# Six gate tiles in the half-size block instead of four, another layout of k and q in DRAM, and a later product with the softmax reciprocals

## The chip, the cores and the metric

The kernel runs on one core of a Trainium2 chip. The metric is the device time of one execution in microseconds, median of several runs: 974.61 us before (three runs, 974.07 to 975.96). A profile of one more execution is read beside it. The engines are TensorE (PE; PEld is its weight load), VectorE (DVE), ScalarE (ACT), GpSimd (POOL) and SyncE (SP), which only issues DMAs here.

## The reference

One layer of a bidirectional encoder on 512 tokens of width 2048. One projection gives q, k, v and a gate for two groups of 16 heads of 64; group A attends with three dilated windows that share a bias table, group B to a 2-D neighbourhood on an 8 x 64 grid. Gated outputs go through the output projection, and the result is normalised with the scaled input.

```python
h = jnp.einsum('bsd,de->bse', x, w_in[layer])
qa, ka, va, ga, qb, kb, vb, gb = jnp.split(h, splits, axis=-1)
ya = _dilated_attention(heads(qa, N_HEADS_A), heads(ka, N_HEADS_A), heads(va, N_HEADS_A), t5_bias)
yb = _neighbourhood_attention(heads(qb, N_HEADS_B), heads(kb, N_HEADS_B), heads(vb, N_HEADS_B), na_rpb[layer])
ya = merge(ya) * jax.nn.silu(ga.astype(jnp.float32))
yb = merge(yb) * jax.nn.silu(gb.astype(jnp.float32))
y = jnp.concatenate([ya, yb], axis=-1).astype(x.dtype)
out = jnp.einsum('bse,ed->bsd', y, w_out[layer])
x = _layer_norm(DEEPNORM_ALPHA * x + out, ln_gain[layer], ln_bias[layer])
```

## The kernel before

Everything is float32, and each product is made of three TensorE passes on rounded high and low parts: high x high, high x low, low x high. ScalarE makes a high part with a copy, VectorE the low part with a subtraction.

**Stages.** First `plain_block` computes the first four of 16 gate tiles (a tile is 128 gate columns, the gate of one pair of heads) while x arrives. Then `strassen_block` computes k, q and v of both groups, one block for each kind and group, with Strassen's scheme: seven products of half-size matrices instead of eight. Between k and q of group B stands a block of kind "s", with half-size operands, for the next `MID` = 4 gate tiles. The other eight gate tiles are computed later, as fillers in the attention loop.

**Units.** A block's products are cut into units of weights. A unit is loaded by SP (`load`), summed with another unit where the product needs it (`add`, VectorE), split into a high part (`high`, ScalarE) and a low part (`low`, VectorE), and multiplied (`run`, TensorE). `run_blocks` lays them out by hand: at unit n it issues the sum of unit n+3, the split of n+2 and the matmuls of n; `behind` holds what else is due there, such as the combining of products, the stores, and the loads, which go out some units ahead (`base - ahead`). A k or q result leaves in eight pieces (`store_kq`), each turned by TensorE, split, and stored to DRAM by SP. PE, DVE and ACT follow this order as written; SP's order is made by the scheduler, in one queue for loads and stores.

**The loop.** Each of the 16 pairs of heads (groups alternate) has eight steps, four for a head of 128 queries each. At step n the loop (lines 813 to 851) issues: the scores of n (two matmuls into a bank of the pool `pss`, which has two banks); the softmax's first instruction on VectorE (s, with the row minimum) and the exponential on ScalarE; the transposes of step n-2 (`turn`), which ScalarE and VectorE copy out as th and tl; and at n % 4 == 2 the value matmuls of the head before (`values`, into the same pool), which ScalarE copies (tmp) and VectorE adds (y). Between these it puts matmuls that need nothing of the step, the fillers: `fill(amount)` takes them from the remaining gate tiles and then from the first half of the output projection (`out_first`). In a step, half of `amount` goes ahead of `turn`, the rest behind. `later` puts a task behind a step; VectorE's tasks of steps with n % 4 == 1 are held until the next step's softmax has been issued (`held`).

**A pair's y.** `share` (n % 8 == 1 of the next pair) turns the softmax sums' reciprocals and sends them through DRAM (`rc_d`) to a tile rc, `gate` (n % 8 == 4) multiplies y by the gate, and `gated` (n % 8 == 7) by rc, and then makes y's high (ScalarE) and low part (VectorE) for the output projection, one step after the other. `load_kq`, `load_v`, `load_sg` and `load_bias` fetch what the next pair needs; k's high and low parts lie on the two halves of the partitions, q's high part is put there twice, and its low part (`ql`) lies beside zeros.

Of the kernel before, what the change touches and what calls it, by code (L numbers as in the profile page):

```python
# [64 lines left out]
ORDER = [(m % 2, m // 2) for m in range(2 * PAIRS)]  # L65
EARLY, MID = 4, 4
AWAKE = 9
# [4 lines left out]
def hybrid_layer(tc, xT, xn, w_in, w_early, w_mid, w_gate, w_out, t5x, brow, rpb, cmask, eye, gain, lbias, out):  # L72
    nc = tc.nc
    from contextlib import ExitStack
    with ExitStack() as ctx:
# [154 lines left out]
        def store_kq(kind, g, ch, half, b, src):  # L230

            o = vst.next("kst", F32R)
            hi, lo = o[:, 0:512], o[:, 512:1024]
            if kind == "k":
                split(src, hi, lo)
            else:
                nc.scalar.activation(hi, src, AF.Copy, scale=-0.125)
                nc.vector.scalar_tensor_tensor(lo, src, -0.125, f(hi), op0=ALU.mult, op1=ALU.subtract)
            o = o.rearrange("p (s n q) -> p s n q", s=2, n=2)
            for n in range(2):  # L240
                for i in range(2):
                    if kind == "k":
                        to = k_d[g][4 * ch + 2 * b + n].rearrange("s c a q -> c s a q")[:, :, i]
                        nc.sync.dma_start(to[:, :, HALF * half:HALF * half + HALF], f(o[64 * i:64 * i + 64, :, n]))
                    else:
                        to = q_d[g][4 * ch + 2 * b + n][i].rearrange("c (b h q) -> c h b q", b=4, h=2)[:, half]
                        nc.sync.dma_start(to, f(o[:, i, n].rearrange("p (b q) -> p b q", b=4)))

# [102 lines left out]
        def strassen_block(src, kind, g, hooks):  # L351

            base = len(jobs)
            units, tiles = (2, 1) if kind == "s" else (4, 2)

            def load(q, tags):
                def run():
                    for u in range(units):
                        raw = slot(tags[u], F32, "braw")
                        nc.sync.dma_start(raw, src[units * q + u])  # L360
                        raws[q].append(raw)
                return run
# [3 lines left out]
            def product(i, pool, q, other=None, onto=None):  # L366
# [7 lines left out]
                def high(u):  # L374
                    h = halves.next("wh", F32R)
                    nc.scalar.activation(h, raws[q][u], AF.Copy)  # L376
                    return h

                def low(u, h):
                    l = halves.next("wl", F32R)  # L380
                    nc.vector.tensor_tensor(l, raws[q][u], f(h), ALU.subtract)  # L381
                    return h, l

                def run(u, h, l):
                    if u == 0 and first:
                        accs.extend(bank(pool, "acc") for _ in range(tiles))
                    if kind == "s":
                        for kk in range(4):
                            k = 4 * u + kk
                            ah, al = operand(i, k)  # L390
                            for n in range(2):
                                c = slice(256 * kk + 128 * n, 256 * kk + 128 * n + 128)
                                o = accs[0][:, HALF * n:HALF * n + HALF]
                                nc.tensor.matmul(o, h[:, c], ah, start=first and k == 0 and n == 0, stop=False, skip_group_check=skip)
                                nc.tensor.matmul(o, h[:, c], al, start=False, stop=False, skip_group_check=skip)
                                nc.tensor.matmul(o, l[:, c], ah, start=False, stop=k == 7 and n == 1, skip_group_check=skip)
                    for t in range(2 if kind != "s" else 0):
# [24 lines left out]
            def pair(name):  # L422
                if name not in made:
                    t = temps.next(name)
                    made[name] = [t[:, :512], t[:, 512:]]
                return made[name]
# [8 lines left out]
            tags = list(sets)  # L435
            if kind == "s":
                for q, ahead, i, m in ((0, 6, 0, 0), (1, 5, 0, 2), (3, 3, 1, 0), (2, 0, 1, 2)):
                    behind.setdefault(base - ahead, []).append(load(q, tags[i][m:m + 2]))
            else:
                for q, ahead, i in ((0, 6, 0), (1, 4, 1), (3, 2, 2)):  # L440
                    behind.setdefault(base - ahead if base else -4, []).append(load(q, tags[i]))
                at(2, 2, load(2, tags[1]))

# [29 lines left out]
            def put(name, ch, half, t):  # L473
                o = p1[t] if name == "c11" else pair(home[name])[t]
                if kind == "v":
                    store_v(g, ch, half, t, o)
                    return
                sg = vst.next("sg")[:, :512]
                silu(sg, o)
                for n in range(2):  # L480
                    nc.sync.dma_start(sg_d[EARLY + 2 * ch + n][:, HALF * half:HALF * half + HALF], sg[:, HALF * n:HALF * n + HALF])

# [323 lines left out]
        with tc.manual_schedule(engines=engines):  # L806
# [224 lines left out]
def _weights(w_in, w_out):  # L1031
# [20 lines left out]
    for i in range(2):  # L1052
        for j in range(2):
            a = np.concatenate([w[8 * i:8 * i + 8, :, c:c + 128] for c in gate[EARLY + 2 * j:EARLY + 2 * j + 2]], axis=2)
            mid.append(a.reshape(2, 4, 128, 256).transpose(0, 2, 1, 3).reshape(2, 128, 1024))
    return (np.concatenate(blocks), early, np.concatenate(mid), np.concatenate([narrow(c) for c in gate[EARLY + MID:]]),
# [37 lines left out]
```

## Time and profile before

| | |
|---|---|
| median of 3 runs | 974.61 us (974.07 to 975.96) |
| the profiled execution: its own time | 975.21 us |
| its span in the profile | 973.4 us |
| TensorE / VectorE / ScalarE / GpSimd instructions | 4789 / 1144 / 857 / 323 |
| DMA | 194.18 MB, mean 199 GB/s |

The profile covers one execution. Busy times of an engine are given per stage in windows counted from the span's start. Matmuls overlap, so that the mean duration of one is not the time that it takes out of TensorE's queue; for that, starts are compared. "<-" names what ended an idle time.

### The profile page before, as it was taken

The numbers are of one execution on the slowest core, as the hardware profiler recorded it, in microseconds if no ns is written. First come the engines' busy times: TensorE is split into PE (matmuls) and PEld (weight loads), VectorE is DVE, ScalarE is ACT, GpSimd is POOL, SyncE is SP. The second block draws the span as 40 slices with busy tenths as digits, with TensorE's granted clock in tenths as the row PEclk, the third lists the DMA queues.
The fourth block names the chain that finished last, engine by engine and source line by source line (L and its number), as shares of the span: only waits on it lengthen the run. The fifth ranks groups of instructions, "written<-read, shape, count | busy, mean of one in ns | idle before, by whom it ended". The sixth has DMA issues, their size and how long they took to land. (4 is left out here: it accounts for less than half of the span.)

```text
span 973.4 us, 13993 instructions
## 1 busy us (share of the span) xinstructions
PE 964.3 (99%) x4789; PEld 803.6 (83%) x4789; DVE 757.0 (78%) x1144; ACT 496.3 (51%) x857; POOL 181.3 (19%) x323
## 2 busy tenths in 40 slices
PE   8999999999999999999999999999999999999997
PEld 6887888888888889988888888888888888888886
DVE  7897778679789777796788856777776777777877
ACT  7454444444444344443445446776766766672300
POOL 1006656835636000000000000011111000100020
PEclk9999999999999999999999999999999999999999
DMA  9715796698396087420872687887887678779213
GB/s 336 277 65 133 229 329 210 171 296 235 107 350 207 33 282 206 163 93 17 266 182 103 206 271 209 224 234 212 236 239 218 204 228 204 209 219 314 91 58 117
DMA packets 120263, 194.18 MB, mean 199 GB/s; under 512 B 49455, under 2 KB 69807, under 8 KB 120192
## 3 DMA queue, kind: packets, MB, share of 16 engines
q1 hardware_dynamic: 107520, 169.68, 57.3%
q0 software_dynamic: 12096, 22.95, 8.5%
q8 instruction: 38, 0.62, 0.3%
q10 hardware_dynamic: 576, 0.66, 0.2%
q14 instruction: 33, 0.27, 0.1%
HBM read 148.69 MB, written 44.50 MB: 198 GB/s over the span
## 5 line engine op out<-in xcount | busy, mean ns | idle before, releaser
L376 ACT ACTIVATE wh<-braw 128x1024 fp32r<-128x1024 f32 x182 | 193.3, 1062 | 269.2 <-PE acc L404 206.5
L381 DVE TENSOR_TENSOR wl<-braw,wh 128x1024 fp32r<-128x1024 f32 x182 | 223.6, 1230 | 53.8 <-ACT wh L376 53.6
L403 PE MATMUL acc<-wh,xk 128*128 128x512 f32 x384 | 151.3, 394 | 0.0
L405 PE MATMUL acc<-wl,xk 128*128 128x512 f32 x384 | 149.7, 390 | 0.0
L404 PE MATMUL acc<-wh,xk 128*128 128x512 f32 x384 | 149.5, 389 | 0.0
L372 DVE TENSOR_TENSOR braw<-braw 128x1024 f32<-128x1024 f32 x104 | 126.6, 1217 | 0.1
L403 PE MATMUL acc<-wh,op 128*128 128x512 f32 x288 | 113.1, 393 | 0.0
L405 PE MATMUL acc<-wl,op 128*128 128x512 f32 x288 | 112.2, 390 | 0.0
L404 PE MATMUL acc<-wh,op 128*128 128x512 f32 x288 | 112.1, 389 | 0.0
L756 PE MATMUL acc<-wh,yk 128*128 128x512 f32 x320 | 108.1, 401 | 0.0
L692 DVE TENSOR_TENSOR tl<-pt,th 128x256 fp32r<-128x256 f32 (+1 forms) x128 | 71.0, 555 | 35.8 <-ACT th L691 34.1
L691 ACT ACTIVATE th<-pt 128x256 fp32r<-128x256 f32 (+1 forms) x128 | 62.3, 489 | 47.6 <-PE pt L686 45.4
L403 PEld LDWEIGHTS acc<-wh,xk 128*128 128x128 f32 x384 | 72.1, 188 | 15.3 <-ACT bias L151 0.9
L405 PEld LDWEIGHTS acc<-wl,xk 128*128 128x128 f32 x384 | 72.1, 188 | 15.2
L404 PEld LDWEIGHTS acc<-wh,xk 128*128 128x128 f32 x384 | 72.2, 188 | 14.5
L627 ACT ACTIVATE p<-s,mn 128x512 f32<-128x512 f32 (+1 forms) x96 | 62.2, 648 | 29.4 <-DVE mn L623 29.0
L623 DVE CUSTOM_DVE_ANT_0 s<-sc,biases 128x512 f32<-128x512 f32 (+2 forms) x128 | 67.7, 529 | 10.8 <-PE sc L667 10.0
L562 PE MATMUL acc<-xk,wh 128*128 128x512 f32 x256 | 75.3, 404 | 0.0
L756 PEld LDWEIGHTS acc<-wh,yk 128*128 128x128 f32 x320 | 58.5, 189 | 8.8
L161 POOL DMA_DIRECT2D bias<-rows_d x128 | 61.6, 489 | 17.6 <-DMA biasa_d<-bias 5.5
L756 PE MATMUL acc<-wl,yk 128*128 128x512 f32 x160 | 63.9, 403 | 0.0
L405 PEld LDWEIGHTS acc<-wl,op 128*128 128x128 f32 x288 | 54.1, 188 | 11.4
(188 smaller groups left out, 1708.2 us busy)
## 6 DMA issues: line engine op xcount, KB each, us to landing
braw<-in_w_in SPq DMA_DIRECT2D x96, 512.0 KB
wraw<-in_w_out SPq DMA_DIRECT2D x32, 512.0 KB
k_d<-kst SPq DMA_DIRECT2D x64, 128.0 KB
q_d<-kst SPq DMA_DIRECT2D x64, 128.0 KB
v_d<-vst SPq DMA_DIRECT2D x32, 256.0 KB
q<-q_d SPq DMA_DIRECT2D x32, 256.0 KB
wraw<-in_w_gate SPq DMA_DIRECT2D x16, 512.0 KB
k<-k_d SPq DMA_DIRECT2D x16, 512.0 KB
```

The source lines that it names most:

```text
L372: nc.vector.tensor_tensor(raws[q][u], raws[q][u], raws[other][u], ALU.add)
L376: nc.scalar.activation(h, raws[q][u], AF.Copy)
L381: nc.vector.tensor_tensor(l, raws[q][u], f(h), ALU.subtract)
L403: nc.tensor.matmul(accs[t], ah[:, q], h[:, c], start=first and k == 0, stop=False, skip_group_check=skip)
L404: nc.tensor.matmul(accs[t], al[:, q], h[:, c], start=False, stop=False, skip_group_check=skip)
L405: nc.tensor.matmul(accs[t], ah[:, q], l[:, c], start=False, stop=k == 7, skip_group_check=skip)
L562: nc.tensor.matmul(acc, w[:, k * 128:k * 128 + 128], X[8 * u + k][:, s], start=u == 0 and n == 0 and k == 0, stop=u == 1 and n == 2 and k ...
L623: nc.vector.tensor_tensor_reduce(*flat, bias, 1.0, 3e38, ALU.add, ALU.min, mn)
L627: nc.scalar.activation(p[:, to:to + n].rearrange("p (b r c) -> p b r c", r=8, c=c), s[:, :n].rearrange(order, r=8, c=c), AF.Exp, bias=mn, ...
L691: nc.scalar.activation(th, pt[:, :nch], AF.Copy)
L692: nc.vector.tensor_tensor(tl, pt[:, :nch], f(th), ALU.subtract)
L756: nc.tensor.matmul(acc[:, part], yk[k][:, s, c], w[:, wk], start=first and kk == 0 and n == 0, stop=last and kk == 1 and n == 2)
```

## The change

- `MID` goes from 4 to 6: the block "s" computes six gate tiles, and six are left as fillers. The block's units become four per product with 2 x 384 columns instead of two with 4 x 256, and a result has two accumulators (512 and 256 wide). Its loads go out at the same units as those of the other blocks.
- In DRAM k's high and low parts, and q's two heads, lie next to each other for each of the 64 channels. A pair's k is one load as before, q's high part one load on 128 partitions (each row read twice) instead of two on 64, and ql a load onto every second partition, of a tile that is zero elsewhere. A piece of q is stored by eight DMAs of 64 partitions instead of four of 128.
- The fillers are 6, 5, 1, 4 in each four steps until step 75 and 8, 6, 1, 6 then (before: 8, 6, 1, 6 until step 63 and 8, 7, 1, 7). In steps with n % 4 == 1 until step 75 one filler, not half, stands ahead of the transposes.
- `gated` runs at n % 8 == 1 of the pair after the next, two steps later, but for the last two pairs.

```diff
-EARLY, MID = 4, 4
+EARLY, MID = 4, 6
...
-        k_d = [dram.tile([PAIRS, 2, 64, 2, S], F32, name=f"k{g}_d") for g in range(2)]
-        q_d = [dram.tile([PAIRS, 2, 128, S], F32, name=f"q{g}_d") for g in range(2)]
+        k_d = [dram.tile([PAIRS, 64, 2, 2, S], F32, name=f"k{g}_d") for g in range(2)]
+        q_d = [dram.tile([PAIRS, 2, 64, 2, S], F32, name=f"q{g}_d") for g in range(2)]
...
                     else:
-                        to = q_d[g][4 * ch + 2 * b + n][i].rearrange("c (b h q) -> c h b q", b=4, h=2)[:, half]
-                        nc.sync.dma_start(to, f(o[:, i, n].rearrange("p (b q) -> p b q", b=4)))
+                        to = q_d[g][4 * ch + 2 * b + n][i].rearrange("c a (b h q) -> c a h b q", b=4, h=2)[:, :, half]
+                        for a in range(2):
+                            nc.sync.dma_start(to[:, a], f(o[64 * a:64 * a + 64, i, n].rearrange("p (b q) -> p b q", b=4)))
...
-            units, tiles = (2, 1) if kind == "s" else (4, 2)
+            units, tiles = 4, 2
+            cols, wide = (128 * MID // 2, (512, HALF * (MID // 2 - 2))) if kind == "s" else (512, (512, 512))
...
-                        for kk in range(4):
-                            k = 4 * u + kk
+                        for kk in range(2):
+                            k = 2 * u + kk
                             ah, al = operand(i, k)
-                            for n in range(2):
-                                c = slice(256 * kk + 128 * n, 256 * kk + 128 * n + 128)
-                                o = accs[0][:, HALF * n:HALF * n + HALF]
...
+                            for n in range(MID // 2):
+                                c = slice(cols * kk + 128 * n, cols * kk + 128 * n + 128)
+                                o = accs[n // 2][:, HALF * (n % 2):HALF * (n % 2) + HALF]
...
-            nc.gpsimd.memset(f(ql[64:128]), 0.0)
+            nc.gpsimd.memset(f(ql), 0.0)
...
-            nc.sync.dma_start(f(kt.rearrange("p a n -> p (a n)")), k_d[g][j].rearrange("s c a q -> (s c) (a q)"))
-            for n, to in enumerate((qt[0:64], qt[64:128], ql[0:64])):
-                nc.sync.dma_start(f(to), q_d[g][j][n // 2].rearrange("(a c) q -> c a q", a=2))
+            nc.sync.dma_start(f(kt.rearrange("p a n -> p (a n)")), k_d[g][j].rearrange("c s a q -> (c s) (a q)"))
+            nc.sync.dma_start(f(qt.rearrange("p a n -> p (a n)")), _view(q_d[g], j * 256 * S, [[2 * S, 64], [0, 2], [1, 2 * S]]))
+            nc.sync.dma_start(f(ql[0:128:2].rearrange("p a n -> p (a n)")), q_d[g][j][1].rearrange("c a q -> c (a q)"))
...
-                amount = ((8, 6, 1, 6) if n < 64 else (8, 7, 1, 7))[b]
+                amount = ((6, 5, 1, 4) if n < 76 else (8, 6, 1, 6))[b]
+                ahead = 1 if b == 1 and n < 76 else amount // 2
...
-                    fill(amount // 2)
+                    fill(ahead)
...
-                    fill(amount - amount // 2)
+                    fill(amount - ahead)
...
-                if n >= 8 and n % 8 == 7:
+                if n % 8 == 1 and 2 <= i < 2 * PAIRS:
+                    gated(i - 2)
+                if n % 8 == 7 and i >= 2 * PAIRS - 1:
                     gated(i - 1)
```

Line numbers behind the first edit are up to three apart before and after. Three places of the built program show how instructions move.

SP's queue in the stretch in which the block q of group A ends and v begins; `kst` is a piece of q, `braw` are weights. Before:

```order
L360 DMA braw<-in_w_in 128x1024 x6
L247 DMA q_d<-kst 512x1x64 x4
L360 DMA braw<-in_w_in 128x1024
L247 DMA q_d<-kst 512x1x64 x4
L360 DMA braw<-in_w_in 128x1024 x7
L247 DMA q_d<-kst 512x1x64 x4
L360 DMA braw<-in_w_in 128x1024
L247 DMA q_d<-kst 512x1x64 x4
L360 DMA braw<-in_w_in 128x1024
L247 DMA q_d<-kst 512x1x64 x16
L360 DMA braw<-in_w_in 128x1024 x4
```

and now:

```order
L362 DMA braw<-in_w_in 128x1024 x6
L248 DMA q_d<-kst 64x4x64 x16
L362 DMA braw<-in_w_in 128x1024 x2
L248 DMA q_d<-kst 64x4x64 x8
L362 DMA braw<-in_w_in 128x1024 x4
L248 DMA q_d<-kst 64x4x64 x8
L362 DMA braw<-in_w_in 128x1024 x4
L248 DMA q_d<-kst 64x4x64 x32
L362 DMA braw<-in_w_in 128x1024 x4
```

Ahead of the ninth to twelfth of these weight loads stood eight q stores; now 24 smaller ones stand there.

TensorE in a step with n % 8 == 1 of the loop, from its scores to the next step's value matmuls; `acc` rows are fillers, the `pt` rows with `biases` the transposes. Before:

```order
L667 MATMUL sc<-k,ql 128x512
L562 MATMUL acc<-xk_111,wl 128x512
L562 MATMUL acc<-xk_112,wl 128x512
L562 MATMUL acc<-xk_113,wl 128x512
L686 MATMUL pt<-ident,biases 128x128 x2
L562 MATMUL acc<-xk_98,wh 128x512
L562 MATMUL acc<-xk_99,wh 128x512
L562 MATMUL acc<-xk_100,wh 128x512
L717 MATMUL pt<-ident,den 8x128
L666 MATMUL sc<-k,q 128x512
L667 MATMUL sc<-k,ql 128x512
L708 MATMUL pv<-th,vv 128x256 x3
```

and now:

```order
L666 MATMUL sc<-k,ql 128x512
L561 MATMUL acc<-xk_105,wl 128x512
L685 MATMUL pt<-ident,biases 128x128 x2
L561 MATMUL acc<-xk_106,wh 128x512
L561 MATMUL acc<-xk_107,wh 128x512
L561 MATMUL acc<-xk_108,wh 128x512
L561 MATMUL acc<-xk_109,wh 128x512
L716 MATMUL pt<-ident,den 8x128
L665 MATMUL sc<-k,q 128x512
L666 MATMUL sc<-k,ql 128x512
L707 MATMUL pv<-th,vv 128x256 x3
```

One filler instead of three stands ahead of the transposes, and four instead of three between them and the value matmuls that read their copies.

VectorE around the start of a pair of group A; `ISA s,mn` is the softmax's first instruction, the row with `rc` the product with the reciprocals, the row with `pv` the addition behind the value matmuls. Before:

```order
L739 TENSOR_TENSOR y<-y,rc 128x512
L623 ISA s,mn<-sc,biases 128x512
L623 ISA mn 128x1
L692 TENSOR_TENSOR tl<-pt,th 128x256
L844 RECIPROCAL den<-den 128x8
L623 ISA s,mn<-sc,biases 128x512
L623 ISA mn 128x1
L692 TENSOR_TENSOR tl<-pt,th 128x256
L623 ISA s,mn<-sc,biases 128x512
L623 ISA mn 128x1
L548 TENSOR_TENSOR wl<-wraw,wh 128x1024
L741 SCALAR_TENSOR_TENSOR yk<-y,yk 128x512
```

and now:

```order
L622 ISA s,mn<-sc,biases 128x512
L622 ISA mn 128x1
L691 TENSOR_TENSOR tl<-pt,th 128x256
L622 ISA s,mn<-sc,biases 128x512
L622 ISA mn 128x1
L738 TENSOR_TENSOR y<-y,rc 128x512
L833 TENSOR_TENSOR y<-pv,tmp 64x512
L691 TENSOR_TENSOR tl<-pt,th 128x4x128
L622 ISA s,mn<-sc,biases 128x512
L622 ISA mn 128x1
L691 TENSOR_TENSOR tl<-pt,th 128x4x128
L740 SCALAR_TENSOR_TENSOR yk<-y,yk 128x512
```

The product with rc has moved from in front of the pair's first softmax to behind its third, directly ahead of the addition of y; y's low part (`yk`) has moved from there to behind the fourth step's tl.

More of the change, by code (lines that the diff above doesn't have):

```diff
@@ L358, in run @@
                     for u in range(units):
[L359 removed]
+                        raw = slot(tags[u], F32, "braw")[:, :2 * cols]
                         nc.sync.dma_start(raw, src[units * q + u])
@@ L374, in high @@
                 def high(u):
-                    h = halves.next("wh", F32R)
+                    h = halves.next("wh", F32R)[:, :2 * cols]
                     nc.scalar.activation(h, raws[q][u], AF.Copy)
@@ L379, in low @@
                 def low(u, h):
-                    l = halves.next("wl", F32R)
+                    l = halves.next("wl", F32R)[:, :2 * cols]
                     nc.vector.tensor_tensor(l, raws[q][u], f(h), ALU.subtract)
@@ L385, in run @@
                     if u == 0 and first:
-                        accs.extend(bank(pool, "acc") for _ in range(tiles))
+                        accs.extend(bank(pool, "acc")[:, :n] for n in wide)
                     if kind == "s":
-                        for kk in range(4):
-                            k = 4 * u + kk
+                        for kk in range(2):
+                            k = 2 * u + kk
                             ah, al = operand(i, k)
-                            for n in range(2):
-                                c = slice(256 * kk + 128 * n, 256 * kk + 128 * n + 128)
-                                o = accs[0][:, HALF * n:HALF * n + HALF]
-                                nc.tensor.matmul(o, h[:, c], ah, start=first and k == 0 and n == 0, stop=False, skip_group_check=skip)
+                            for n in range(MID // 2):
+                                c = slice(cols * kk + 128 * n, cols * kk + 128 * n + 128)
+                                o = accs[n // 2][:, HALF * (n % 2):HALF * (n % 2) + HALF]
+                                nc.tensor.matmul(o, h[:, c], ah, start=first and k == 0 and n % 2 == 0, stop=False, skip_group_check=skip)
                                 nc.tensor.matmul(o, h[:, c], al, start=False, stop=False, skip_group_check=skip)
-                                nc.tensor.matmul(o, l[:, c], ah, start=False, stop=k == 7 and n == 1, skip_group_check=skip)
+                                nc.tensor.matmul(o, l[:, c], ah, start=False, stop=k == 7 and (n % 2 == 1 or n == MID // 2 - 1),
+                                                 skip_group_check=skip)
                     for t in range(2 if kind != "s" else 0):
@@ L424, in pair @@
                     t = temps.next(name)
-                    made[name] = [t[:, :512], t[:, 512:]]
+                    made[name] = [t[:, :512], t[:, 512:512 + wide[1]]]
                 return made[name]
@@ L435, in strassen_block @@
             tags = list(sets)
[L436 to L442, printed above, removed]
+            for q, ahead, i in ((0, 6, 0), (1, 4, 1), (3, 2, 2)):
+                behind.setdefault(base - ahead if base else -4, []).append(load(q, tags[i]))
+            at(2, 2, load(2, tags[1]))
             def keep(t):
@@ L477, in put @@
                     return
-                sg = vst.next("sg")[:, :512]
+                sg = vst.next("sg")[:, :wide[t]]
                 silu(sg, o)
-                for n in range(2):
-                    nc.sync.dma_start(sg_d[EARLY + 2 * ch + n][:, HALF * half:HALF * half + HALF], sg[:, HALF * n:HALF * n + HALF])
+                for n in range(wide[t] // HALF):
+                    nc.sync.dma_start(sg_d[EARLY + MID // 2 * ch + 2 * t + n][:, HALF * half:HALF * half + HALF], sg[:, HALF * n:HALF * n + HALF])
             for t in range(tiles):
```

7 lines of the change are left out of this document (4 added, 3 removed).

## The prediction

> **What bounds the kernel now.** I read the page's busy times first, then the chain that ended last, then busy time by stage, and last who waits for whom inside the attention stage.
>
> ```profile
> PE 964.3 (99%) x4789; PEld 803.6 (83%) x4789; DVE 757.0 (78%) x1144; ACT 496.3 (51%) x857; POOL 181.3 (19%) x323
> PE 26%; DVE 1%; ACT 1%; issue 1%; DMA 1%; DVEq 0%; POOL 0%; ACTq 0%
> ```
>
> TensorE is busy for 964.3 of 973.4 us, and the chain of waits that can be followed back is nearly all TensorE too. A busy share says nothing about rate, because matmuls overlap. So I looked for stages in which TensorE waits at all.
>
> ```profile
> core 0: us, PE busy (x) PEld busy (x) DVE busy (x) ACT busy (x) POOL busy (x), PEclk, DMA share, GB/s
> 50.00:367.00 317.00, 317.00 (x1434) 260.91 (x1433) 256.40 (x257) 144.95 (x168) 140.34 (x252) 1.00 0.67 205
> 367.00:409.00 42.00, 42.00 (x351) 41.87 (x351) 31.69 (x34) 18.79 (x22) 0.00 (x0) 1.00 0.63 192
> 409.00:563.00 154.00, 154.00 (x696) 127.47 (x695) 126.09 (x130) 72.27 (x85) 1.90 (x2) 1.00 0.48 142
> 576.00:720.00 144.00, 143.78 (x782) 119.31 (x781) 105.71 (x252) 99.86 (x238) 15.26 (x28) 1.00 0.82 229
> 720.00:880.00 160.00, 159.83 (x867) 133.09 (x866) 117.86 (x272) 108.67 (x257) 13.35 (x26) 1.00 0.76 215
> ```
>
> The stages are the projection blocks (50 to 563, with the half-size gate block at 367 to 409) and the attention loop's first 64 steps and the rest (576 to 880). TensorE is covered everywhere, at a granted clock of 1.00. So a change gains what it takes out of TensorE's queue, and loses what it makes TensorE wait. VectorE has the least room: 256 of 317 us in the blocks, 106 of 144 in the loop.
>
> **The change part by part. First, the move of two gate tiles.** In the half-size block the sum over k runs through 7 products of 8 k-tiles, and each column chunk of 128 takes 3 matmuls on 256 positions (high x high, high x low, low x high). Four tiles are 2 chunks, 7 x 8 x 2 x 3 = 336 matmuls; six are 3 chunks, 504. As a filler a tile is 48 matmuls on 512 positions, so 96 of these go.
>
> ```profile
> L394 PE MATMUL acc<-xk,wh x64: 278/283/364, 367.6 to 408.5; 128*128 128x256 f32 x64
> L396 PE MATMUL acc<-xk,wl x64: 279/283/283, 367.9 to 408.8; 128*128 128x256 f32 x64
> 690.37 0.44 PE pt L686 x4
> 880.31 15.67 PE acc L756 x69
> ```
>
> The durations of 283 ns overlap and can't be used. From the first start to the last there are 41.2 us; one more interval, less two bursts of four transposes for the k block before it (0.44 us each by the like burst of the chain), leaves 40.4 us for 336: 0.1205 us each. On 512 positions the chain has 69 in 15.67 us: 0.227 each, and fillers cost the same. The block grows by 168 x 0.1205 = 20.2 us, the fillers shrink by 96 x 0.227 = 21.8 us (22.1 at 0.23): **-1.7 us**. This is the whole arithmetic gain. A tile costs 10.1 us in the block and 10.9 as a filler; at the long matmul's rate seven products for eight would give 9.5, but a short one costs 6% more per element.
>
> The Trainium skill, page "TensorE: Matmul & The Clock Gate", section "Back-to-back issue gap", puts the gap at N/2.4 + 2.5 ns, 109 ns for 256 columns and 216 for 512. By it the block would grow by 18.3 us and the fillers shrink by 20.7: -2.4 us. The rows here are 10 and 5% above the page, so their -1.7 is used.
>
> Can the block hold that pace? A unit of weights is now 768 wide instead of 1024 and has 18 matmuls, 2.17 us, where it had 24, 2.89 us.
>
> ```profile
> L381 DVE TENSOR_TENSOR wl<-braw,wh 128x1024 fp32r<-128x1024 f32 x14 | 17.0, 1218 | 2.2 <-ACT wh L376 2.2
> L372 DVE TENSOR_TENSOR braw<-braw 128x1024 f32<-128x1024 f32 x104 | 126.6, 1217 | 0.1
> L89 DVE TENSOR_TENSOR wl<-wraw,wh 128x512 fp32r<-128x512 f32 x15 | 10.3, 684 | 0.8 <-ACT wh L88 0.7
> ```
>
> At 768 wide an instruction lies halfway between 684 and 1218, 0.95 us by estimate. The block then has 28 low parts and 16 sums, 42 us, and 18 combining and gating steps of at most 0.7 us each: 54 of its 60.7 us. A unit with a sum needs 1.9 of 2.17 us; the projection blocks run at 2.43 of 2.72 (12 x 0.227) with no wait of TensorE. So I cost the pace at nothing, hidden by work prepared two units ahead. If that cover went, each of the 16 units with a sum could last 0.2 us longer: +3 us. The bytes are the same: the weights of two tiles, four loads of 512 KB, move from the gate stream to the block. The zero fill of 128 partitions instead of 64 is on GpSimd, which is idle there.
>
> **Second, the loop with fewer fillers.** The 49 fillers of the prologue stay. Steps 0 to 75 have 16 per four steps instead of 21 (22 from step 64), and the rest 21 instead of 22. In the first 64 steps that is 80 fillers, 18.2 us less cover. VectorE loses only 80/24 = 3.3 low parts of 1.2 us and one gate product, some 4.7 us. From 105.7 of 144 us it goes to about 101 of 126, so 25 us of idle time are left. What is its idle time now?
>
> ```profile
> engine line waited for: us in total, times, longest us
> DVE tl L692 <- ACT th L691: 16.8, 24, 1.2
> DVE y L833 <- ACT tmp L832: 16.2, 14, 1.7
> DVE s L623 <- PE sc L667: 7.7, 4, 6.0
> DVE y L739 <- DMA rc<-rc_d: 1.2, 2, 0.6
> ```
>
> 33 us are waits for ScalarE's th and tmp, latencies that don't shrink with the fillers. 33 into 25 doesn't go: some 8 us must vanish because VectorE arrives later, or become waits of TensorE. This bounds the new stalls of these steps: 0 to 8 us. Where they would come is seen at one step:
>
> ```profile
> 617.75 0.48 PE L666 MATMUL sc<-k,q 128*128 128x512 f32 x1
> 618.86 0.69 DVE L833 TENSOR_TENSOR y<-pv,tmp 64x512 f32<-64x512 f32 x1 [1.02 <-ACT tmp L832]
> 619.58 0.69 DVE L692 TENSOR_TENSOR tl<-pt,th 128x512 fp32r<-128x512 f32 x1
> 620.12 0.40 PE L666 MATMUL sc<-k,q 128*128 128x512 f32 x1
> 620.19 0.68 DVE L568 SCALAR_TENSOR_TENSOR sgo<-sgo,acc 128x512 f32<-128x512 f32 x1
> 620.78 0.68 DVE L623 CUSTOM_DVE_ANT_0 s<-sc,biases 128x512 f32<-128x512 f32 x1
> ```
>
> y ends at 619.55 and frees the bank that the scores at 620.12 write: 0.57 us to spare. The step between loses two fillers, 0.46 us, so 0.11 is left. Behind the waiting scores stand every later matmul and filler. The scores of 617.75 are taken up 3.0 us later, at 620.78; with steps 0.46 us shorter such lateness grows. The edit that issues one filler, not three, ahead of the second step's transposes gives th two fillers more room, at the one place where TensorE waits for it. Today VectorE runs 3 us late and TensorE loses a few tenths, so I choose near the low end: **+1.6 us** for the loop.
>
> **Third, y times the reciprocals two steps later.**
>
> ```profile
> 680.11 5.90 DMA rc<-rc_d
> 686.03 0.69 DVE L739 TENSOR_TENSOR y<-y,rc 128x512 f32<-128x512 f32 x1 [0.55 <-DMA rc<-rc_d]
> 686.64 0.68 DVE L623 CUSTOM_DVE_ANT_0 s<-sc,biases 128x512 f32<-128x512 f32 x1
> 688.60 0.28 PE L708 MATMUL pv<-th,vv 128*128 128x256 f32 x1
> 689.03 0.63 PE L708 MATMUL pv<-th,vv 128*128 128x256 f32 x3 [0.15 <-ACT th L691]
> ```
>
> The reciprocals land at 686.0, VectorE stands 0.55 us for them, the softmax behind starts late, and a value matmul on 256 positions, due 0.12 us after its neighbour, comes after 0.43: 0.3 us lost. It happens twice in the 16 pairs. Two steps later the DMA is long home. The product also moves into the place where VectorE waits for tmp, while the low part of y moves out of it, to the step before a head starts: no net work moves. I take **-0.8 us** for these and the smaller waits they cause (0 to -1.2). The product ends well before the output projection's fourth unit reads pair 7 at step 77.
>
> **Fourth, k and q in DRAM.** Loads: two of q instead of three for each pair, in rows of 4 KB; they are issued a pair, eight steps, ahead, and that hides them: nothing. If that failed, a pair's scores would wait, but the loads get fewer. Stores of q: eight issues a piece instead of four.
>
> ```profile
> L247 SPq DMA_DIRECT2D q_d<-kst x64: 512/637/3278, 188.9 to 506.3; - x64
> L244 SPq DMA_DIRECT2D k_d<-kst x64: 574/599/1179, 109.6 to 387.3; - x64
> 188.93 2.87 SPq L247 DMA_DIRECT2D q_d<-kst  x4
> 192.57 4.41 SPq L247 DMA_DIRECT2D q_d<-kst  x4
> 197.07 5.27 SPq L360 DMA_DIRECT2D braw<-in_w_in  x7
> 202.43 6.66 SPq L247 DMA_DIRECT2D q_d<-kst  x4
> 215.02 1.22 DVE L372 TENSOR_TENSOR braw<-braw 128x1024 f32<-128x1024 f32 x1
> ```
>
> A half store still has three dimensions like the k store, so about 0.6 us each: 4 x 0.6 = 2.4 us more on SP for each of the eight pieces. The order of SP's queue shows what stands behind: the weight loads of the next block's second set, now in the run of seven from 197.07, come after the third piece, that is after 24 stores. That piece's stores begin at 202.43 today; eight at 0.6 us, or 6.7 us if the queue holds them up as now, end at 207 to 209. VectorE sums the first of these weights at 215.02, and TensorE uses them three units after the sum. So it is hidden, by 6 us less a landing time that SP's rows don't show (the rc load took 5.9). I cost it at nothing, and at +4 us if that cover goes (below).
>
> The Trainium skill, page "DMA: Bandwidth & Descriptors", section "Rules for kernel authors", says that two transfers to disjoint partition halves serialise and that one over 128 partitions is to be used. It speaks for the new q load and against the halved q store: by it the sum would take the +4 us of the rival on SP, by the rows nothing; no run yet shows either.
>
> Sum: -1.7 + 1.6 - 0.8 = **-0.9 us**, made against the profiled execution of 975.21 us (span 973.4, and 1.8 around it); that one lies 0.6 above the median of 974.61, to which I apply the difference: **973.7 us**.
>
> **The rivals.** *The waits vanish freely* (VectorE simply arrives later, as it does today): -1.7 - 0.8 and nothing given back, at most -1.7 - 1.2: 971.7 to 972.1. For it speaks that TensorE hardly waits at 3 us of lateness; against it the 0.11 us of the bank.
>
> *VectorE binds the early loop*, the slower side: from the point where y ends over 0.57 us later than at 619.55, or th arrives behind the value matmuls, each head of the first 19 stalls by 0.2 to 0.4 us. At two thirds of the bound of 8 us: -2.5 + 5.3 = +2.8: 977.4. For it speaks 33 into 25, against it that group-B heads, with scores 192 or 256 wide, let VectorE catch up.
>
> *SP falls behind in the q blocks*: if the first load lands 4 us after 207 to 209 and later ones queue with 24 stores, the block starts late by up to 2 us, twice: +4 on top of -0.9: 977.7.
>
> *The change doesn't do what it says*: the block misses its pace, +3 on top of the forecast, and the two tiles bring nothing: 976.7.
>
> **How the numbers follow.** Forecast 973.7 with 0.46; no new stalls 0.30; VectorE binds 0.15; SP 0.06; pace 0.03. About 0.2%, 1.9 us, is what a measurement tells from no change. Faster by more is the second case, 0.30. Within it lies the forecast and the milder end of the SP case, 0.47. Slower is the rest, 0.23. The range from 971.4 to 977.4 takes in the second case and reaches the third's centre.
>
> **What would show it.** Right: 504 matmuls of 256 positions in some 61 us; no wait for rc; a loop some 21 us shorter, with new waits of scores or value matmuls below 2 us; VectorE near 80% in steps 0 to 63. Wrong: a wait of TensorE in a block that follows q; a loop shorter by 18 us or less; units of the gate block over 2.2 us apart.

## The result, and the profile after

The changed kernel takes 983.84 us (median of 6 runs, 982.21 to 985.46) beside 974.21 us (973.51 to 975.96) for the kernel before on the same chip: ratio 1.0097, 95% interval 1.0082 to 1.0111. By the ratio it is 9.4 us slower, outside the range given. Its profiled execution took 982.71 us, with a span of 980.9 us, 7.5 above the span before; it is 1.1 us below its kernel's median and the one before 1.0 above, so the traces show some 2 us less than the medians.

The page's busy times and the windows by stage, as in the prediction (the half-size block is now 368 to 430, the loop begins at 598):

```profile
PE 966.4 (99%) x4861; PEld 805.3 (82%) x4861; DVE 769.1 (78%) x1169; ACT 502.4 (51%) x870; POOL 187.9 (19%) x321
```
```profile
50.00:368.00 318.00, 316.84 (x1432) 260.38 (x1431) 253.89 (x254) 143.82 (x167) 148.33 (x252) 1.00 0.67 202
368.00:430.00 62.00, 62.00 (x518) 61.95 (x517) 50.86 (x65) 29.31 (x41) 0.00 (x0) 1.00 0.55 173
430.00:585.00 155.00, 154.32 (x694) 126.97 (x693) 126.45 (x132) 71.95 (x86) 1.91 (x2) 1.00 0.49 146
598.00:720.00 122.00, 119.41 (x661) 98.08 (x660) 93.90 (x227) 90.26 (x217) 12.96 (x24) 1.00 0.76 240
720.00:881.00 161.00, 158.28 (x865) 130.34 (x864) 121.57 (x290) 112.76 (x271) 14.77 (x28) 1.00 0.72 214
```

The share of 99% tells nothing. The stages do: TensorE's column falls short of the window's length by 1.2 and 0.7 us in the projection blocks and by 2.6 and 2.7 us in the loop, where before it was covered everywhere. The half-size block is full. What TensorE waits for, from the view of waits (line and releaser, us in total, times, longest; rows of the opening and of the end are left out):

```profile
PE pv L707 <- ACT th L690: 3.7, 4, 1.1
PE acc L408 <- DVE wl L383: 1.8, 3, 1.2
PE pv L707 <- DVE mn L622: 0.8, 1, 0.8
PE pv L707 <- issue: 0.4, 1, 0.4
PE sc L665 <- DVE mn L622: 0.3, 2, 0.2
```

There are two losses: value matmuls (pv) and scores in the loop, 5.2 us (before: 0.2), and projections (acc L408), 1.8 us (before: none). Starts of consecutive matmuls, which also show waits too short for this view, give 7.1 and 2.7 us more than before. With the arithmetic's -1.7 and an opening (up to 50 us) shorter by 0.7 that is 7.4 of the 7.5 us. Of the loop's 7.1, 3.1 stand in steps 0 to 63, 1.8 in steps 64 to 75 and 2.2 behind them.

**The loop.** VectorE around the longest of these waits, that of the value matmuls of step n % 8 == 6 in a pair of group A (timeline: start, duration, line; in brackets the idle time before and what ended it), then TensorE and ScalarE there:

```profile
637.96 0.69 DVE L691 TENSOR_TENSOR tl<-pt,th 128x512 fp32r<-128x512 f32 x1 [0.55 <-ACT th L690]
638.57 1.22 DVE L547 TENSOR_TENSOR wl<-wraw,wh 128x1024 fp32r<-128x1024 f32 x1
639.70 0.69 DVE L740 SCALAR_TENSOR_TENSOR yk<-y,yk 128x512 fp32r<-128x512 f32 x1
640.30 0.68 DVE L622 CUSTOM_DVE_ANT_0 s<-sc,biases 128x512 f32<-128x512 f32 x1
...
640.91 0.69 DVE L691 TENSOR_TENSOR tl<-pt,th 128x512 fp32r<-128x512 f32 x1
641.52 0.68 DVE L730 TENSOR_TENSOR y<-y,sg 128x512 f32<-128x512 f32 x1
642.11 0.68 DVE L622 CUSTOM_DVE_ANT_0 s<-sc,biases 128x512 f32<-128x512 f32 x1
```
```profile
638.66 0.40 PE L665 MATMUL sc<-k,q 128*128 128x512 f32 x1
...
641.05 0.50 PE L665 MATMUL sc<-k,q 128*128 128x512 f32 x1 [0.17 <-DVE mn L622]
641.39 0.40 PE L666 MATMUL sc<-k,ql 128*128 128x512 f32 x1
642.91 1.17 PE L707 MATMUL pv<-th,vv 128*128 128x512 f32 x4 [1.12 <-ACT th L690]
```
```profile
641.09 0.72 ACT L626 ACTIVATE p<-s,mn 128x512 f32<-128x512 f32 x1 [1.98 <-DVE mn L622]
...
641.81 0.58 ACT L690 ACTIVATE th<-pt 128x512 fp32r<-128x512 f32 x1
```

From 637.96 VectorE works without a gap: the low part of a weight unit, y's low part (`yk`, which the change moved here), the softmax of step n % 8 == 4, its tl, the gate's product, the softmax of step 5. That last one reads the scores of 638.66 only at 642.11, 3.5 us after they began. The value matmuls need the bank that it reads, and start 0.12 us after it ends. The th that the row names was late for the same reason: ScalarE had itself waited 1.98 us for VectorE's row minimum of step 4.

**The blocks.** The first of the three waits of `acc`, in the block v of group A: SP's queue, then ScalarE and VectorE.

```profile
188.23 12.08 SPq L248 DMA_DIRECT2D q_d<-kst  x16
200.35 1.09 SPq L362 DMA_DIRECT2D braw<-in_w_in  x2
201.55 5.50 SPq L248 DMA_DIRECT2D q_d<-kst  x8
207.09 2.29 SPq L362 DMA_DIRECT2D braw<-in_w_in  x4
209.48 7.69 SPq L248 DMA_DIRECT2D q_d<-kst  x8
217.21 2.25 SPq L362 DMA_DIRECT2D braw<-in_w_in  x4
```
```profile
230.15 0.60 ACT L237 ACTIVATE kst<-pt 128x512 fp32r<-128x512 f32 x1 [3.62 <-DMA q_d<-kst]
```
```profile
230.78 0.69 DVE L238 SCALAR_TENSOR_TENSOR kst<-pt,kst 128x512 fp32r<-128x512 f32 x1 [3.60 <-DMA q_d<-kst]
231.39 1.22 DVE L383 TENSOR_TENSOR wl<-braw,wh 128x1024 fp32r<-128x1024 f32 x1
```

A piece of q waits for a staging tile (`kst`, one of three) that an earlier store has not yet emptied, because the stores stand in SP's queue; behind the piece in VectorE's order stands the weights' low part, and TensorE waits 1.2 us for that.

### The profile page after: what moved, and what is told of

Its sections match the earlier page's. It is cut to its first block, busy times and chain, and to the rows that moved or that the text cites. A ratio compares the mean times of both kernels' runs of the same rounds, so it can differ in the third digit from the quotient of the medians.

```text
span 980.9 us, 14280 instructions
## 1 busy us (share of the span) xinstructions
PE 966.4 (99%) x4861; PEld 805.3 (82%) x4861; DVE 769.1 (78%) x1169; ACT 502.4 (51%) x870; POOL 187.9 (19%) x321
## 4 chain that ended last, share of the span: by engine, by line
PE 87%; DMA 4%; ACT 3%; DVE 3%; issue 2%; SPq 1%; DVEq 0%; ACTq 0%
PE acc L755 14%; PE acc L408 14%; PE acc L406 14%; PE acc L407 14%; PE acc L561 6%; PE pv L707 4%; PE pt L685 3%; PE acc L396 2%; PE acc L398 2%; PE acc L397 2%; PE sc L666 2%; PE sc L665 2%; PE acc L280 1%; PE sc L755 1%; PE acc L281 1%
## 5 line engine op out<-in xcount | busy, mean ns | idle before, releaser
L378 ACT ACTIVATE wh<-braw 128x1024 fp32r<-128x1024 f32 (+1 forms) x196 | 202.0, 1031 | 276.9 <-PE acc L407 204.5
L383 DVE TENSOR_TENSOR wl<-braw,wh 128x1024 fp32r<-128x1024 f32 (+1 forms) x196 | 233.3, 1192 | 56.8 <-ACT wh L378 56.6
L408 PE MATMUL acc<-wl,xk 128*128 128x512 f32 x384 | 149.7, 390 | 0.0
L374 DVE TENSOR_TENSOR braw<-braw 128x1024 f32<-128x1024 f32 (+1 forms) x112 | 133.1, 1189 | 0.0
L408 PE MATMUL acc<-wl,op 128*128 128x512 f32 x288 | 112.6, 391 | 1.8 <-DVE wl L383 1.8
L755 PE MATMUL acc<-wh,yk 128*128 128x512 f32 x320 | 110.5, 402 | 0.0
L408 PEld LDWEIGHTS acc<-wl,xk 128*128 128x128 f32 x384 | 72.1, 188 | 15.2
L408 PEld LDWEIGHTS acc<-wl,op 128*128 128x128 f32 x288 | 54.0, 188 | 14.4 <-DVE wl L383 3.1
L407 PEld LDWEIGHTS acc<-wh,op 128*128 128x128 f32 x288 | 54.1, 188 | 10.9
```

Of the source, the lines that this page charges most:

```text
L374: nc.vector.tensor_tensor(raws[q][u], raws[q][u], raws[other][u], ALU.add)
L407: nc.tensor.matmul(accs[t], al[:, q], h[:, c], start=False, stop=False, skip_group_check=skip)
L408: nc.tensor.matmul(accs[t], ah[:, q], l[:, c], start=False, stop=k == 7, skip_group_check=skip)
L755: nc.tensor.matmul(acc[:, part], yk[k][:, s, c], w[:, wk], start=first and kk == 0 and n == 0, stop=last and kk == 1 and n == 2)
```

## The experiments

All times are medians beside runs of the kernel before on the same chip, with the ratio and its 95% interval; 0.001 is about 1 us. The kernel before takes 975.1 to 975.4 us there. The theory at the start (T1) put the loop's loss on the new place of y's low part.

**Which part costs what.** Four kernels undo parts of the change (mid_only undoes both that mid_kq and mid_gated undo):

```diff
# mid_kq: the later product undone
-                if n % 8 == 1 and 2 <= i < 2 * PAIRS:
-                    gated(i - 2)
-                if n % 8 == 7 and i >= 2 * PAIRS - 1:
+                if n >= 8 and n % 8 == 7:
# mid_gated: the layout of k and q undone
-        q_d = [dram.tile([PAIRS, 2, 64, 2, S], F32, name=f"q{g}_d") for g in range(2)]
+        q_d = [dram.tile([PAIRS, 2, 128, S], F32, name=f"q{g}_d") for g in range(2)]
...
# kq_gated: six tiles and new amounts undone
-EARLY, MID = 4, 6
+EARLY, MID = 4, 4
...
-                amount = ((6, 5, 1, 4) if n < 76 else (8, 6, 1, 6))[b]
+                amount = ((8, 6, 1, 6) if n < 64 else (8, 7, 1, 7))[b]
```

> The changed kernel with the product with the reciprocals (and y's high and low part) back at n % 8 == 7 of the next pair, where it was before. Theory T1 (the loop loses because y's low part now stands at the end of step n % 8 == 3, in the part of the pair where VectorE is late already and the thinner fillers give no cover): most of the loop's 7 us of TensorE waits go, 977 us (975 to 979). Rival R1 (the later place costs by itself, whatever the cover): 975 to 976. Rival R2 (the thinner fillers alone cost it): 983, as the changed kernel, or a little more, since the waits for rc come back.

> The changed kernel with k and q in DRAM, their stores and loads as before. If the doubled q stores on SP's queue hold up the weight loads of the blocks v, TensorE's waits in these blocks (2.3 us in the changed kernel's profile) go and the time is 981.5 to 982 us; if they do not, it stays at 983.8. The loop's waits stay by every theory.

> Only the two tiles moved and the fillers' new amounts; k and q, and the product with the reciprocals, as before. T1: 975 us (973 to 977), the two parts' gains added. R2: 981 to 982, since the thinner loop alone makes the waits. If both parts of the change that are left out were free, 983.8.

> The kernel before with the new layout of k and q and the later product, but four tiles in the half-size block and the fillers' old amounts. T1 (the later place costs only where the cover is thin): 976 to 977 us, the 2 us of the q stores alone. R1: 981 to 983, since the later place costs wherever it stands. R2: 976, the same as T1, less the waits for rc.

And a fifth makes the later product alone:

> The kernel before with the later product alone; fillers, tiles, k and q as before. If the layout of k and q is all that the kernel with both cost (its waits of 3.6 us in the blocks, its loop as long as before's): 975.4 us, the same as before. The prediction's step on the product: 974.6. If the later place costs by itself: 978.8.

| kernel | tiles and fillers | layout of k, q | later product | us | ratio to before (95%) |
|---|---|---|---|---|---|
| changed | yes | yes | yes | 983.84 | 1.0097 (1.0082 to 1.0111) |
| mid_kq | yes | yes | no | 987.27 | 1.0122 (1.0106 to 1.0138) |
| mid_gated | yes | no | yes | 980.26 | 1.0052 (1.0039 to 1.0064) |
| mid_only | yes | no | no | 987.71 | 1.0128 (1.0113 to 1.0143) |
| kq_gated | no | yes | yes | 978.81 | 1.0040 (1.0027 to 1.0053) |
| gated_only | no | no | yes | 974.83 | 0.9997 (0.9989 to 1.0006) |

T1 and R1 fall: undoing the later product makes the thin loop slower, not faster. R2 is left, but it had 981 to 983, and the two kernels take 987. The tiles with the thinner loop lose 12.5 us by themselves. The later product takes back 7.4 of that with the old layout, but only 2.4 with the new one (1.0122 against 1.0097, the intervals just overlap), and beside the old fillers it does nothing that can be measured. The layout costs 4.2 us beside the old fillers (1.0040 against 0.9997) and 4.4 in the changed kernel (1.0097 against 1.0052), more than the 2 us that the expectations had from the view of waits.

Without the later product the layout seems free (1.0122 against 1.0128), but it is not: the starts of matmuls show 4.5 us more of gaps in mid_kq's blocks than in mid_only's, and 3.9 us fewer in its loop. Some 3 of these 3.9 us are, by estimate, a lower granted clock of mid_only's TensorE after a long wait (last section); the four runs of mid_only have a mean clock of 0.994 to 0.997, those of mid_kq 0.997 to 0.999. Why VectorE's longest wait for rc is 3.6 us in mid_only and 1.8 in mid_kq is not shown.

Why the old place of the product costs so much in the thin loop is read in mid_only, in VectorE's timeline and the windows around it (TensorE's busy time is the second number, PEclk the third from the end):

```profile
745.14 0.69 DVE L690 TENSOR_TENSOR tl<-pt,th 128x512 fp32r<-128x512 f32 x1
749.47 0.69 DVE L737 TENSOR_TENSOR y<-y,rc 128x512 f32<-128x512 f32 x1 [3.64 <-DMA rc<-rc_d]
```
```profile
748.50:752.00 3.50, 0.81 (x5) 0.33 (x3) 1.98 (x7) 1.52 (x4) 0.00 (x0) 1.00 1.05 235
752.00:754.00 2.00, 0.98 (x2) 0.83 (x3) 1.00 (x4) 1.61 (x5) 0.10 (x1) 0.53 0.83 179
754.00:756.00 2.00, 2.00 (x6) 1.57 (x5) 1.77 (x4) 0.60 (x2) 0.43 (x1) 0.50 0.24 72
756.00:758.00 2.00, 2.00 (x8) 1.60 (x8) 0.54 (x1) 0.84 (x2) 1.00 (x2) 0.50 0.00 0
758.00:760.00 2.00, 2.00 (x11) 1.57 (x10) 1.18 (x5) 0.88 (x4) 0.05 (x1) 0.76 0.42 139
760.00:762.00 2.00, 2.00 (x12) 1.64 (x11) 0.86 (x5) 0.89 (x4) 0.00 (x0) 1.00 0.99 340
```
```profile
DVE y L737 <- DMA rc<-rc_d: 6.0, 4, 3.6
```

The six steps between the reciprocals and the product got shorter, the DMA hardly (the load of rc lands after 5.3 us in the median, 5.9 before, and took 9.0 in the wait shown): VectorE waits 6.0 us for rc in four pairs instead of 1.2 us in two.

**Is VectorE what TensorE waits for in the loop?** Base mid_gated. Two kernels move work of VectorE out of the stretch without a gap, one moves fillers into it:

```diff
# low_later
-        later(2, lambda: nc.vector.scalar_tensor_tensor(t[:, 1], y, 0.5, f(t[:, 0]), op0=ALU.mult, op1=ALU.subtract), True)
+        later(4 if i % 2 == 0 and i < 14 else 2, lambda: nc.vector.scalar_tensor_tensor(t[:, 1], y, 0.5, f(t[:, 0]), op0=ALU.mult, op1=ALU.subtract), True)
# low_gate_later: that, and
-                    later(0, lambda i=i: gate(i - 1), True)
+                    later(1 if i % 2 == 0 and i < 2 * PAIRS else 0, lambda i=i: gate(i - 1), True)
# fill_shift: mid_gated, and
                 amount = ((6, 5, 1, 4) if n < 76 else (8, 6, 1, 6))[b]
+                if i % 2 == 0 and i < 2 * PAIRS:
+                    amount += (-1, -1, 0, 0, 1, 2, 0, -1)[n % 8]
```

> Base: the changed kernel with k and q as before (980.3 us beside 975.4 of before). Only y's low part is moved in the pairs of group A: from the end of step n % 8 == 3 to step n % 8 == 6, behind the softmax and ahead of y, where VectorE waits up to 1.65 us for tmp. Theory T2 (in these pairs VectorE works without a gap from the end of step 3 to the softmax of step 5, whose reading frees the bank of the value matmuls, so that each instruction of 0.61 us that leaves this stretch takes as much out of TensorE's wait): the waits of 0.6 to 1.6 us in seven pairs shrink by 0.6 us each, 976 to 977.5 us. Rival R2 (with fewer fillers ScalarE's latencies, th and tmp, show at TensorE whatever VectorE does): no change, 980.3.

> As the run before, and the product of y with the gate also moved, from the end of step n % 8 == 4 to the same place in step n % 8 == 6, in the pairs of group A. T2: another 0.6 us in each pair where a wait is left, 975 us (974 to 976.5). R2: 980.3. If the place is filled by then, y comes later, frees its bank later, and the time is that of the run before or 1 us above it.

> Base: the changed kernel with k and q as before (ratio 1.0052 to the kernel before, 980.3 us). Only fillers change place, in the pairs of group A: one each from the steps n % 8 = 0, 1 and 7 to the steps 4 (one) and 5 (two), so that the same number stands in a pair. T2 (VectorE is late only in steps 3 to 5 of these pairs; TensorE's cover counts where VectorE works without a gap): three fillers, 0.68 us, come off each wait of the value matmuls at n % 16 = 6, five times, and 976.5 to 977.5 us. Rival (what counts is the number of fillers, a pair's VectorE work against a pair's length): the waits appear in the steps that lost a filler, 980.

Measured: low_later 978.51 us, 1.0033 (1.0021 to 1.0045); low_gate_later 976.84, 1.0021 (1.0009 to 1.0034); fill_shift 977.48, 1.0020 (1.0011 to 1.0029), each beside 1.0052 of their base. Of the 5.2 us that TensorE waits in the loop of mid_gated, 3.6, 1.8 and 2.8 us are left; in low_gate_later these two rows:

```profile
PE pv L706 <- ACT th L689: 1.0, 2, 0.5
PE pv L706 <- DVE mn L621: 0.8, 1, 0.8
```

T2 holds in the main: with the same fillers, fewer instructions in the stretch or more fillers over it take most of the wait away, and R2 would have left 980.3. The gains (1.9, 3.0 and 3.1 us) are smaller than T2 had them, and low_later and low_gate_later miss its ranges. By the starts only five pairs of group A had a wait over 0.2 us, not seven, and in one of them R2 is right: in low_later VectorE, rid of y's low part, waits for ScalarE's th instead, and TensorE's wait there stays at 0.5 us.

```profile
668.99 0.69 DVE L690 TENSOR_TENSOR tl<-pt,th 128x512 fp32r<-128x512 f32 x1 [0.64 <-ACT th L689]
```

**Has group B cover to give?** On low_gate_later, four fillers of each pair of group B go to the pair of A beside it (16 fillers per head become 18 in A and 14 in B):

```diff
+                if n < 72:
+                    amount += ((0, 0, 0, 0, 2, 2, 0, 0) if i % 2 == 0 else (-1, -1, 0, 0, -1, -1, 0, 0))[n % 8]
```

> As the run with y's low part and the gate's product in step n % 8 == 6, but with four fillers of each pair of group B moved to the pair of group A beside it (20 and 12 per pair-half become 18 and 14 per head), until step 71. If the pairs of group B have room on VectorE (busy 11.3 to 12.5 of 14.3 to 14.6 us): A's waits go, 975 us. If they are as full as A's: their 8 steps last 13.6 instead of 14.5 us only with waits of 0.3 to 0.9 us in each, 977 to 979.

979.98 us, 1.0048 (1.0035 to 1.0060): 2.6 us worse than its base, and above both cases of the expectation. TensorE's waits of this kernel begin with

```profile
PE pt L715 <- DVE den L845: 1.9, 2, 1.2
PE pv L706 <- DVE mn L621: 1.4, 3, 0.5
```

The first row is new: the transposes of the softmax sums wait for VectorE's reciprocals, at the start of a pair of B. By the starts, A's waits up to step 71 are gone, and four pairs of B have new ones of 0.6 to 1.3 us. B has no cover to give in these steps.

**The queue or the transfers?** The changed kernel, with the second half of each q store on GpSimd's queue:

```diff
-                            nc.sync.dma_start(to[:, a], f(o[64 * a:64 * a + 64, i, n].rearrange("p (b q) -> p b q", b=4)))
+                            (nc.sync if a == 0 else nc.gpsimd).dma_start(to[:, a], f(o[64 * a:64 * a + 64, i, n].rearrange("p (b q) -> p b q", b=4)))
```

> The changed kernel, with one of the two halves of each q store issued by GpSimd's queue, so that SP issues as many q stores as before. If SP's queue is what the new layout costs (weight loads behind the doubled stores): TensorE's waits in the blocks v go, 980.3 us, as with the layout of before. If it is the transfers (two half stores on 64 partitions instead of one on 128, in the same DMA engines): 983.8 to 984.8, as the changed kernel.

980.80 us, 1.0055 (1.0043 to 1.0067), against 1.0052 with the old layout, and `acc` waits for no low part any more. The same transfers of 64 partitions, the same bytes, and the whole cost of the layout is gone (its blocks have no more gaps than those of before): it was SP's queue. How much of it is SP's own time for a store and how much its queue being held up, the runs don't separate: the last 32 half stores of the block q of group A take SP 25.6 us in the changed kernel, the 16 whole ones 16.5 us before.

**Does a version beat both?** all_shift joins fill_shift and low_gate_later; all_both also drops the condition on group A in the two moves (but for y's low part of pair 7).

```diff
# all_both, beside all_shift
-        later(4 if i % 2 == 0 and i < 14 else 2, lambda: nc.vector.scalar_tensor_tensor(t[:, 1], y, 0.5, f(t[:, 0]), op0=ALU.mult, op1=ALU.subtract), True)
+        later(4 if i != 7 and i < 14 else 2, lambda: nc.vector.scalar_tensor_tensor(t[:, 1], y, 0.5, f(t[:, 0]), op0=ALU.mult, op1=ALU.subtract), True)
-                    later(1 if i % 2 == 0 and i < 2 * PAIRS else 0, lambda i=i: gate(i - 1), True)
+                    later(1 if i < 2 * PAIRS else 0, lambda i=i: gate(i - 1), True)
```

> The shift of fillers together with y's low part and the gate's product in step n % 8 == 6 (the second run of the set before, ratio 1.0021). T2: of the waits of TensorE that are left in the loop's profile (0.67, 0.23, 0.20, 0.93, 0.66, 0.23 us) those of group A's pairs go, 1.5 to 2 us less: 975 us beside 975.1 of before (974.3 to 975.8), ratio 0.999 to 1.0005. Rival: 976.8 again.

> As the run with the shifted fillers and with y's low part and the gate's product in step n % 8 == 6 (ratio 0.9998), with these two moved in the pairs of group B as well. T2: the wait of 0.93 us at step 46, the last that the profile shows of this kind, goes, and with it 0.9 us: ratio 0.999, 974.0 to 974.8 us beside 975.2 of before; in the block nothing changes. If the place in group B's step 6 has no room, y comes later there and the ratio is 1.000 to 1.003.

all_shift: 974.81 us, 0.9998 (0.9989 to 1.0007). all_both: 975.72, 1.0007 (0.9995 to 1.0020). No: neither can be told from the kernel before. all_both came out as the second case of its expectation: the wait at step 46 went, and in the loop only this row is left:

```profile
PE sc L664 <- DVE y L834: 0.9, 2, 0.7
```

It is the bank that the prediction named, freed by y, which now comes later. The starts of its matmuls show some 1.8 us more of gaps in the loop than before's (0.7 in waits of over 0.19 us, the rest in smaller ones), which is about the arithmetic gain; both profiled spans are 973.4 us.

## Why the prediction was wrong

**The two tiles: right.** The block's 504 matmuls run as computed:

```profile
L396 PE MATMUL acc<-xk,wh x96: 278/283/365, 368.4 to 429.4; 128*128 128x256 f32 x96
L398 PE MATMUL acc<-xk,wl x96: 278/283/285, 368.7 to 429.7; 128*128 128x256 f32 x96
```

61.3 us from the first start to the last, one interval more and the two bursts less, is 60.5: 0.120 each (the estimate was 0.1205). TensorE waits nowhere in the block, so units of 768 keep the pace. The page "TensorE: Matmul & The Clock Gate" of the Trainium skill, section "Back-to-back issue gap", has 109 ns, by its formula for the gap of an isolated matmul; the measured 120 decides here too.

**The thinner loop: the step that failed, by its size and its place.** The term was +1.6 us; mid_gated, with the arithmetic's -1.7, gives +6.8 (5.1 above before). The bound of 0 to 8 us was for steps 0 to 63, and held there: 3.1 us. The other 4.0 us stand behind step 63, where fillers go too and the sum had no cost of their own. VectorE's load was forecast rightly (busy 100.6 of 128.7 us in steps 0 to 63, forecast 101 of 126). What failed is the choice near the low end, "VectorE runs 3 us late and TensorE loses a few tenths": the idle time was averaged over 126 us, while VectorE is full in one stretch of a pair and idle in another, so its 25 us couldn't be used where it was late. The bank named was the wrong one: not the one that y frees before the scores, but the one that the softmax of step 5 frees before the value matmuls. The other became the limit only when that was relieved (all_both). The rival that VectorE binds was right in kind; it had 5.3 us, all of it in the early loop.

**The later product: not told apart from its term, but misjudged.** -0.8 was forecast; alone it is -0.3 us (-1.1 to +0.6), and no wait for rc is left, as forecast. "No net work moves" counted the work and not its place: the low part of y moved into the step that also makes the low part of a weight unit, and taking it out again brought 1.9 us (low_later). What the sum didn't see is what the wait for rc would have become with shorter steps: beside the thin fillers the product's later place is worth 2.4 us in the changed kernel, and 7.4 with the old layout.

**The layout: cost at nothing, costs 4.2 to 4.4 us.** The rival on SP had the price, 4 us, and was given 0.06; the sign that the prediction named for it, a wait of TensorE in a block that follows q, came. The step that failed followed only the weight loads in SP's queue. They go out at 207.09, where it had them (207 to 209), and are not what TensorE waits for. The stores themselves empty a ring of three staging tiles, and the next piece, with everything behind it on VectorE, waits for that. In the block v of group B it is the reload of x behind the last 32 stores: ScalarE waits 5.17 us for it, VectorE 3.22 for ScalarE, and the two other waits of TensorE in the blocks follow. ScalarE's and VectorE's rows of the changed kernel:

```profile
546.01 0.42 ACT L88 ACTIVATE xk<-xback 128x256 fp32r<-128x256 f32 x1 [5.17 <-DMA xback<-in_xT]
```
```profile
546.46 0.42 DVE L89 TENSOR_TENSOR xk<-xback,xk 128x256 fp32r<-128x256 f32 x1 [3.22 <-ACT xk L88]
```

The Trainium skill, "DMA: Bandwidth & Descriptors", section "Rules for kernel authors", warns against halves of the partitions because they serialise. Its warning came true in the time but not by that cause: q_pool has the halves and not the cost. The section "Issuing engines are not separate DMA queues" says that another issuing engine saves only sequencer time, usually small; here the whole cost went with it.

By the terms: -1.7 + 6.8 + 4.4 = +9.5 us, beside 9.4 measured (the later product is inside the 6.8). This sum closes by the way its two large terms are made, as differences of ratios; what bears it out is the 7.4 of 7.5 us from the starts. There the layout has 2.7 us, less than the 4.2 and 4.5 us of gaps that the blocks of kq_gated and mid_kq have over those of before.

## What to carry to other kernels

Cover that is taken out of a loop is not judged by the loop's mean idle time of the next engine: look for its longest stretch without a gap, list what each instruction there frees, and take cover away elsewhere or move work out of it first. Where steps get shorter, recompute every latency that spans a fixed number of steps, such as a DMA's way through DRAM. And when a store is cut in two, follow the buffer that it empties, not only what is queued behind it; a second issuing queue may be all that is needed.

## What was not expected of the hardware

In mid_only TensorE waited 2.5 us, until 751.3, ran three short matmuls and waited again, for 1.2 us (0.81 of 3.50 us busy, then 0.98 of 2.00). At 752.1, when the second wait was 0.3 us old, the granted clock fell to 0.50 and stayed there until 758.9, in the middle of the loop: 2 us that hold 12 matmuls at 1.00 held 6 and 8. The wait was paid for again after it had ended: TensorE worked from 753.0 to 758.9 at half the clock, 3 us lost by estimate. In mid_kq, where the longest such wait was 1.0 us, the clock stayed at 1.00. The Trainium skill, page "TensorE: Matmul & The Clock Gate", section "Part 1: The HAM clock gate", has half rate after an idle window of about 3.4 us; this case agrees in kind, with 3.3 us between the last of the dense matmuls and the fall, though not all of it was idle.
